# 67 fused pairs in place of 55, and four low parts a group made by an accumulating transfer, in a hybrid encoder layer

## The chip, the cores and the metric

One Trainium2 chip, one core of it. The time of a run is the device time of one execution in microseconds (us). The kernel before takes 1573.97 us, the median of 3 runs (1572.58 to 1574.53). One further execution was taken with the profiler on. Its span, from the first to the last profiled instruction, and its whole time are in the table below.

## The reference

One layer of an encoder: x is 256 rows (tokens) of 4096 numbers, all in float32.

```python
xn = rms_norm(x, norm_g[l])
h = jnp.einsum('bsd,de->bse', xn, w_in[l])              # 4096 -> 7 x 2048
c_val, c_glu, c_gate, q, k, v, a_gate = jnp.split(h, split_pts, axis=-1)
conv_out = conformer_conv(c_val, c_glu, ...) * jax.nn.silu(c_gate)   # 31 taps, LayerNorm, swish
q = rms_norm(q.reshape(B, S, 16, 128), q_norm_g[l])
k = rms_norm(k.reshape(B, S, 16, 128), k_norm_g[l])
attn = longnet_mixture(q, k, v, rel_bias)               # three dilated window patterns
attn_out = attn * jax.nn.silu(a_gate)
mixed = jnp.concatenate([conv_out, attn_out], axis=-1)
x = x + jnp.einsum('bse,ed->bsd', mixed, w_out[l])      # 4096 -> 4096
```

Nearly all of the work is in the two einsums: 256 rows times 4096 x 14336 and times 4096 x 4096 weights, 288 MB of weights that are each used once.

## The kernel before

**Groups and pairs.** The weights are cut into 18 column groups of 1024 columns: 14 "input groups" (numbers 0 to 13) and 4 "out groups" (14 to 17). A group is 16 **pairs**. A pair is two blocks of 128 weight rows by the group's 1024 columns, in SBUF one `raw` tile of 128 x 2048 numbers, 1 MB, loaded by one transfer (`load_pair`, L240) that SyncE (SP) issues. There are `RAW` = 3 raw tiles. The load of the pair three places on is issued when all the steps that read a pair's raw tile have been issued, and it waits for them on the chip. `ORDERS[g]` lists the pairs of group g in the order in which they are done; a place in this list is a "slot", and the number 16 g + slot is the pair's unit u.

**Products.** TensorE multiplies in a reduced-precision format (fp32r here). To keep float32 accuracy each weight is split in a high part (a cast on ScalarE, called ACT in the profile) and a low part (raw minus high, a subtraction on VectorE, DVE), and each activation likewise. A product is three matmuls: high·high, low·high and high·low, 128 x 128 by 128 x 512 each. The sums stay in PSUM over the group's 16 pairs.

**Plain pairs** (`split_plain`, `plain`) need 2 row blocks x 2 halves of the tokens x 2 halves of the columns x 3 = 24 matmuls. ACT casts the high part `wh` in two halves (L1022), and DVE subtracts to get `wl` in one operation (L1028). On TensorE (PE) the 16 matmuls with the high part come first (L1195, L1197), then the 8 with the low part (L1195).

**Fused pairs** (`split_fused`, `fused`) use a Strassen scheme (Winograd's form) on the 2 x 2 blocks: seven products in place of eight, so 7 x 3 = 21 matmuls. It needs sums of weight blocks, made by DVE in the raw tile (L1054, L1063, L1064), and their high and low parts: `b` (L1045, L1046), `b22` (L1061, L1062), and two tiles of sums `t1,t3` and `t2,t4` (L1045, L1046). The block sums of the activations are made once (`block_sums`) and kept in tiles of the tag `c4`, of which there are `C4` = 16. The products of all fused pairs of a group also go to four more accumulators m1, m5, m6, m7, and after the group's last fused pair `add_more` (L1232 to L1240) adds these into the group's output tile: one copy on ACT and eight sums on DVE in an out group. Fused pairs are five in each of the input groups 2 to 7, four in group 14, and seven in each of the groups 15 to 17: 30 + 4 + 21 = 55.

**Parts in store.** The parts wait for PE in `W_SLOTS` = 4 tiles of the tag "ws" (128 x 2048), and near fused pairs in up to `W_MORE` = 4 tiles of tag c4 as well. The class `Stream` holds a list `todo` of splitting steps in the order of the units; `before()`, called ahead of each block of matmuls, issues as many of these steps as there is room for in the tiles. So on ACT and DVE the splitting runs ahead of PE by as much as the store holds.

**Fillers.** The rest (the convolution's taps on DVE, its products on ACT through `cp_lane`, block sums, softmax, gates) is cut into steps, and a planner puts them between the splitting steps. For each matmul `credit()` adds 227 ns times a share `FILL` to what DVE and ACT may spend: (0.95, 0.72) in groups with fused pairs, (0.96, 0.93) while taps are being done elsewhere. Each step says what it costs, and `pump()` starts fillers while something is left.

**Attention.** Softmax tiles are turned by a way through DRAM: GpSimd (POOL) issues the write (L391) and the reads that fetch the turned tiles (L398). The products of the last heads (`po`, L740) stand in the first out group, 14. The weights of the out groups begin with the rows that the attention makes last, by an offset of eight pairs in the row number (in `load_pair`).

**End of a group.** The last pair's matmuls are ordered by accumulator (L1210, L1212), so that the four accumulators are done one after the other. In an out group DVE adds each to the output tile `xr` (L826), which a transfer then writes out.

## Time and profile before

| | us |
|---|---|
| median of 3 runs | 1573.97 |
| the profiled execution, whole | 1575.05 |
| its span | 1573.3 |
| TensorE busy (6901 matmul records) | 1565.2 |
| VectorE busy | 1298.7 |
| ScalarE busy | 928.4 |
| GpSimd busy | 99.2 |
| one raw load of 1 MB, issue to landing (median of 286) | 4.9 |

The profiled execution lies 1.08 us over the median, and 1.75 us of it are outside the span. PE is TensorE's matmul, PEld its weight load, SP is SyncE. A row of the timeline gives the start in us, the duration, the engine, the line of the program, the operation, output<-inputs, the shape and how many alike are in the row; in brackets how long the engine stood idle ahead of it and for what. In a list of waits the three numbers are the sum of the waits in us, their count and the longest. Matmuls are pipelined: one issues every 0.23 us, though each is shown with 0.39. The raw loads are all that SP moves besides x and the output; POOL issues transfers only.

### The profile page before, as it was taken

How to read it: one execution, taken by the hardware profiler on the slowest of the kernel's cores; microseconds unless marked ns; L12 is line 12 of the kernel's file. 1: busy time of each engine (PE TensorE's matmuls, PEld its weight loads, DVE VectorE, ACT ScalarE, POOL GpSimd, SP SyncE). 2: the span in 40 equal slices, each digit the busy share in tenths (PEclk: the TensorE clock that was granted, in tenths of full speed). 3: DMA queues.
4: the chain of work that ended last, by engine and by line, in shares of the span. 5: the costliest groups of instructions: out<-in, count | busy, mean ns of one | idle time of the engine just before them, and what ended most of it. 6: DMA issues, size and time to landing. Idle time of an engine off the chain costs nothing.

```text
span 1573.3 us, 18570 instructions
## 1 busy us (share of the span) xinstructions
PE 1565.2 (99%) x6901; PEld 1294.9 (82%) x6901; DVE 1298.7 (83%) x1473; ACT 928.4 (59%) x1421; POOL 99.2 (6%) x184
## 2 busy tenths in 40 slices
PE   9999999999999999999999999999999999999999
PEld 7888888888888888888888888888888788788887
DVE  6667899998989898898878788767566778989897
ACT  6755655566556555667665776665736644555553
POOL 0000000000000000001203023001130300000000
PEclk9999999999999999999999999999999999999999
DMA  9866556555657565656868469556785865666653
GB/s 373 294 226 259 205 211 223 206 209 196 233 184 249 183 248 203 207 210 236 282 207 257 171 247 280 194 194 212 236 272 200 256 222 205 223 241 228 244 221 136
DMA packets 64523, 357.22 MB, mean 227 GB/s; under 512 B 9104, under 2 KB 11920, under 8 KB 27824
## 3 DMA queue, kind: packets, MB, share of 16 engines
q1 hardware_dynamic: 54096, 326.38, 58.6%
q0 software_dynamic: 10048, 29.37, 6.1%
q8 instruction: 54, 0.88, 0.2%
q10 hardware_dynamic: 288, 0.28, 0.1%
q14 instruction: 37, 0.30, 0.1%
HBM read 337.09 MB, written 18.91 MB: 226 GB/s over the span
## 4 chain that ended last, share of the span: by engine, by line
PE 87%; issue 6%; DMA 4%; DVE 1%; ACT 1%; POOL 0%; SPq 0%; DVEq 0%; POOLq 0%; ACTq 0%
PE c L1195 40%; PE c L1197 20%; PE c L1210 3%; PE m L1082 3%; PE m L1080 3%; PE m L1081 3%; PE c L1080 2%; PE c L1081 2%; PE c L1082 2%; PE acc L927 2%; PE acc L924 2%; PE acc L925 2%; PE c L1212 2%; DMA raw<-in_w_dram 1%; PE psc L696 1%
## 5 line engine op out<-in xcount | busy, mean ns | idle before, releaser
L1028 DVE TENSOR_TENSOR wl<-raw,wh 128x2048 fp32r<-128x2048 f32 x217 | 496.4, 2289 | 174.3 <-ACT wh L1022 165.6
L1022 ACT CAST wh<-raw 128x1024 fp32r<-128x1024 f32 x434 | 433.6, 1048 | 255.4 <-PE c L1197 185.1
L1195 PE MATMUL c<-wh,nh 128*128 128x512 f32 x1200 | 467.4, 390 | 0.0
L1197 PE MATMUL c<-wh,nl 128*128 128x512 f32 x1200 | 466.9, 389 | 0.0
L1195 PE MATMUL c<-wl,nh 128*128 128x512 f32 x1200 | 298.2, 391 | 0.0
L1195 PEld LDWEIGHTS c<-wh,nh 128*128 128x128 f32 x1200 | 225.2, 188 | 46.9
L1195 PEld LDWEIGHTS c<-wl,nh 128*128 128x128 f32 x1200 | 225.3, 188 | 46.7
L1197 PEld LDWEIGHTS c<-wh,nl 128*128 128x128 f32 x1200 | 225.2, 188 | 46.7
L1045 ACT CAST t<-raw 128x1024 fp32r<-128x1024 f32 x110 | 115.9, 1054 | 237.2 <-DVE raw L1054 182.7
L1046 DVE TENSOR_TENSOR t<-raw,t 128x1024 fp32r<-128x1024 f32 x110 | 134.2, 1221 | 2.8
L533 DVE SCALAR_TENSOR_TENSOR cT<-a,wT,cT 128x252 f32<-128x252 f32 (+10 forms) x284 | 117.7, 472 | 0.5
L1195 PE MATMUL c<-wh,mh 128*128 128x512 f32 x280 | 109.1, 390 | 0.0
L1197 PE MATMUL c<-wh,ml 128*128 128x512 f32 x280 | 108.9, 389 | 0.0
L495 ACT ACTIVATE cp<-a,wT 128x241 f32<-128x241 f32 (+7 forms) x196 | 84.5, 488 | 9.9 <-DVE cT L524 9.8
L1195 PE MATMUL c<-wl,mh 128*128 128x512 f32 x280 | 69.1, 389 | 0.0
L1054 DVE TENSOR_TENSOR raw<-raw 128x1024 f32<-128x1024 f32 x55 | 67.4, 1225 | 1.9
L1046 DVE TENSOR_TENSOR b<-raw,b 128x1024 fp32r<-128x1024 f32 x55 | 67.0, 1218 | 0.2
L1195 PEld LDWEIGHTS c<-wh,mh 128*128 128x128 f32 x280 | 52.6, 188 | 10.9
L1197 PEld LDWEIGHTS c<-wh,ml 128*128 128x128 f32 x280 | 52.6, 188 | 10.9
L1195 PEld LDWEIGHTS c<-wl,mh 128*128 128x128 f32 x280 | 52.6, 188 | 10.9
L998 DVE TENSOR_TENSOR wh<-raw,wh 128x1024 fp32r<-128x1024 f32 x31 | 37.9, 1224 | 24.8 <-ACT wh L997 24.8
L524 DVE TENSOR_TENSOR cT<-cT,cp 128x964 f32<-128x964 f32 (+7 forms) x49 | 57.1, 1166 | 1.1
(327 smaller groups left out, 2170.6 us busy)
## 6 DMA issues: line engine op xcount, KB each, us to landing
raw<-in_w_dram SPq DMA_DIRECT2D x286, 1024.0 KB, 4.9
xT<-in_x_cols_dram SPq DMA_DIRECT2D x15, 512.0 KB, 8.0
x<-in_x_dram SPq DMA_DIRECT2D x8, 512.0 KB, 8.8
xr<-in_x_dram SPq DMA_DIRECT2D x8, 512.0 KB, 6.5
out_dram<-xr SPq DMA_DIRECT2D x15, 256.0 KB, 6.8
T<-bias_dram SPq DMA_DIRECT2D x16, 192.0 KB, 6.1
raw<-in_w_dram SPq DMA_DIRECT2D x3, 512.0 KB, 6.7
turn_qk0d<-turn_qk POOLq DMA_DIRECT2D x2, 512.0 KB, 5.5
```

The lines of the kernel that those rows point to most:

```text
L495: nc.scalar.activation(cp[:, t, lo:hi], a[:, t, lo + sh : hi + sh], AF.Copy, scale=wT[:, 4 * cb + t, k : k + 1],)
L533: nc.vector.scalar_tensor_tensor(c[:, t, lo:hi], a[:, t, lo + sh : hi + sh], wT[:, 4 * cb + t, k : k + 1], c[:, t, lo:hi], op0=ALU.mult, o ...
L1022: nc.scalar.copy(h, raw_tiles[u][:, k])
L1028: nc.vector.tensor_sub(l, src, h.bitcast(F32))
L1045: nc.scalar.copy(h, src)
L1046: nc.vector.tensor_sub(l, src, h.bitcast(F32))
L1054: nc.vector.tensor_add(r[:, 0:4:3, :], r[:, 0:3:2, :], twice(r[:, 3, :]))
L1080: nc.tensor.matmul(acc, a[0], b[0], start=start, stop=False)
L1081: nc.tensor.matmul(acc, a[1], b[0], start=False, stop=False)
L1082: nc.tensor.matmul(acc, a[0], b[1], start=False, stop=stop)
L1195: nc.tensor.matmul(acc, a[s][0], b[e], start=begin, stop=False)
L1197: nc.tensor.matmul(acc, a[s][1], b[e], start=False, stop=False)
```

## The change

Three things change, and several smaller ones follow from them.

1. **More fused pairs.** In the input groups 2 to 7 pair 12 becomes fused as well (six a group), and in the out groups 15 to 17 pairs 0 to 7 and 9 (nine a group in place of seven): 36 + 4 + 27 = 67. The new pair's block sums use two tiles of a smaller tag (`small`), and `C4` rises to 18, which also holds the two tiles that the convolution's products had for themselves.
2. **Low parts by a transfer.** In the last three groups pairs 10, 11, 12 and 13 are split by `split_by_dma`. The high part is cast as before. The low part is not subtracted on DVE: ACT writes the negated value of raw, rounded to fp32r, into `wl` (L1046 of the new program), and GpSimd issues a transfer that reads the same weights from DRAM again and adds them to it (L1048), in two halves of 512 KB. That is 12 pairs, 24 negations and 24 transfers. PE multiplies the high part after the next fused pair and the low part after the one behind that (`late`). The splitting steps are taken into those of the neighbouring fused pairs (`guest`, `held`).
3. **Order in a fused pair.** The four products of t1 to t4 are done with all high parts first, then with the low parts.

Besides: `add_more` is a row of steps, one taken behind each half of a plain part, where it was done at once; `FILL` rises; the store may hold 7 more tiles in the out groups 15 to 17 (`W_LAST`); the ACT products of the convolution are started behind the `b22` cast where ACT has credit.

```diff
-FILL, SAVED = ((0.95, 0.72), (0.96, 0.93)), (700, 700)
+FILL, SAVED = ((0.97, 0.76), (1.0, 0.93)), (700, 700)
-C4 = 16
+C4 = 18
-FUSED = [(2, 4, 6, 8, 10) if g in FUSED_IN else () for g in range(N_IN)]
-FUSED += [range(4)] + 3 * [range(7)]
+FUSED = [(2, 4, 6, 8, 10, 12) if g in FUSED_IN else () for g in range(N_IN)]
+FUSED += [range(4)] + 3 * [(*range(8), 9)]
-ORDERS += 3 * [(8, 9, 0, 10, 1, 11, 2, 3, 12, 4, 5, 13, 6, 14, 15, 7)]
-W_SLOTS, W_MORE = 4, 4
+ORDERS += 3 * [(8, 10, 0, 1, 11, 2, 3, 12, 4, 5, 13, 6, 7, 9, 14, 15)]
+BY_DMA = (N_IN + 1) * [()] + 3 * [(10, 11, 12, 13)]
+W_SLOTS, W_MORE, W_LAST = 4, 4, 7
...
-    cps = deque((const.tile([P, 4, S], F32, name=f"cp{i}"), 0) for i in range(2))
+    cps = deque((t4(f"cp{i}"), 0) for i in range(2))
...
-        if left[1] > 1500 and not split_gens:
+        if left[1] > 1500 and state["taps"] and not split_gens:
             cp_lane.step(left, spend)
...
+                elif ORDERS[g][slot] in BY_DMA[g]:
+                    make = self.split_by_dma
                 new = [(n, f, u) for n, f in make(u)]
                 self.parts_left[u] = len(new)
+                if make == self.split_by_dma:
+                    guest = new
+                    continue
+                if guest:
+                    new[2:] = [*guest[:2], new[2], guest[2], new[3]]
+                new[1:1], held, guest = held, guest[3:], []
                 self.todo.extend(new)
...
+        def split_by_dma(self, u):
+            g, slot = divmod(u, n_pairs)
+            def low(k):
+                if k == 0:
+                    self.parts[(u, "l")] = self.two(f"wl{u}", (u, "l"))
+                l = self.parts[(u, "l")][k]
+                nc.scalar.activation(l, raw_tiles[u][:, k], AF.Copy, scale=-1.0)
+                src = w[g, row_of(u), :, 1024 * k : 1024 * k + 1024]
+                nc.gpsimd.dma_start(l, src.bitcast(F32R), accum_op=ALU.add)
+                spend(0, 1055)
+            halves = (TWO, lambda: low(0)), (NONE, lambda: low(1))
+            return [*self.split_plain(u)[:2], *halves]
...
                 nc.scalar.copy(h, r[:, 2, :])
+                for _ in range(2):
+                    if left[1] > 800:
+                        cp_lane.step(left, spend)
                 nc.vector.tensor_sub(l, r[:, 2, :], h.bitcast(F32))
...
+                more_now = W_LAST if g > n_in else W_MORE
+                self.more = more_now if firsts and slot + 2 >= firsts[0] else 0
...
                     if last:
-                        self.add_more(g, more)
+                        self.adding = self.add_more(g, more)
+                    if late and late[0] >= u - 2:
+                        self.plain(*late, rows, one, False, "hl"[u - late[0] - 1])
                     continue
...
+                if j in BY_DMA[g]:
+                    late = u, j
+                    continue
...
-                (more["m5"], "s1", "t1", ""), (more["m7"], "s3", "t3", "t13"),
-                (more["m6"], "s2", "t2", ""), (one["c21"], "a22", "t4", "t42"),
...
+            for part in range(2):
+                for acc, an, bn in sums:
+                    self.before()
+                    own = acc is not one["c21"]
+                    (ah, al), b = a[an], self.parts[(u, bn)][part]
+                    begin, end = own and first and part == 0, own and last and part == 1
+                    nc.tensor.matmul(acc, ah, b, start=begin, stop=end)
+                    if part == 0:
+                        nc.tensor.matmul(acc, al, b, start=False, stop=False)
+                    credit((2 - part) * PRODUCT)
```

How this moves the instructions is seen at three places. The first is ACT in the last three groups. Before, in group 17, two fused pairs (units 278 and 279) are followed by a plain one, whose two `wh` casts stand behind all of the fused pairs' casts:

```order
L1045 CAST b_11541<-raw_11463 128x1024
L1061 CAST b_278_11546<-raw_11463 128x512
L1045 CAST t_278_11560<-raw_11463 128x1024
L1045 CAST t_278_11569<-raw_11463 128x1024
L1045 CAST b_11590<-raw_11502 128x1024
L1061 CAST b_279_11594<-raw_11502 128x512
L1045 CAST t_279_11607<-raw_11502 128x1024
L1045 CAST t_2790_11616<-raw_11502 128x1024
L1022 CAST wh_11631<-raw_11533 128x1024 x2
L1045 CAST b_11654<-raw_11572 128x1024
```

After, in group 15, with the by-DMA pair in raw_10434 (unit 247) and the fused pairs 248, 249 and 251 in raw_10423, raw_10465 and raw_10537:

```order
L1084 CAST b_10477<-raw_10423 128x1024
L1100 CAST b_248_10483<-raw_10423 128x512
L1061 CAST wh_10504<-raw_10434 128x1024 x2
L1084 CAST t_2480_10513<-raw_10423 128x1024
L1046 ACTIVATE wl_10520<-raw_10434 128x1024
L1084 CAST t_248_10534<-raw_10423 128x1024
L1084 CAST b_10541<-raw_10465 128x1024
L1046 ACTIVATE wl_10521<-raw_10434 128x1024
L1100 CAST b_249_10562<-raw_10465 128x512
L1084 CAST t_249_10573<-raw_10465 128x1024
L1084 CAST t_2490_10589<-raw_10465 128x1024
L1084 CAST b_10597<-raw_10537 128x1024
```

The by-DMA pair's casts and its two negations now stand inside the splitting of the two fused pairs, and POOL issues the transfer of a half as soon as its negation is done.

The second place is PE inside a fused pair, in the sums t (before, unit 278 of group 17; m are the four more accumulators, msp and mh/ml the parts of the activations):

```order
L1080 MATMUL m_17_11458<-t_278_11560,msp_9626 128x512
L1081 MATMUL m_17_11458<-t_278_11560,msp_9626 128x512
L1082 MATMUL m_17_11458<-t_278_11560,msp_9626 128x512
L1080 MATMUL m_17_11460<-t_278_11560,msp_9626 128x512
L1081 MATMUL m_17_11460<-t_278_11560,msp_9626 128x512
L1082 MATMUL m_17_11460<-t_278_11560,msp_9626 128x512
L1080 MATMUL m_17_11459<-t_278_11569,msp_9626 128x512
L1081 MATMUL m_17_11459<-t_278_11569,msp_9626 128x512
L1082 MATMUL m_17_11459<-t_278_11569,msp_9626 128x512
L1080 MATMUL c_17_11378<-t_278_11569,mh_9592 128x512
L1081 MATMUL c_17_11378<-t_278_11569,ml_9593 128x512
L1082 MATMUL c_17_11378<-t_278_11569,mh_9592 128x512
```

After (unit 251 of group 15; t_2510 holds the high parts of t1 and t3, t_2511 their low parts, t_251 both parts of t2 and t4):

```order
L1237 MATMUL m_15_10327<-t_2510_10631,msp_9855 128x512
L1239 MATMUL m_15_10327<-t_2510_10631,msp_9855 128x512
L1237 MATMUL m_15_10329<-t_2510_10631,msp_9855 128x512
L1239 MATMUL m_15_10329<-t_2510_10631,msp_9855 128x512
L1237 MATMUL m_15_10328<-t_251_10651,msp_9855 128x512
L1239 MATMUL m_15_10328<-t_251_10651,msp_9855 128x512
L1237 MATMUL c_15_10275<-t_251_10651,mh_9821 128x512
L1239 MATMUL c_15_10275<-t_251_10651,ml_9822 128x512
L1237 MATMUL m_15_10327<-t_2511_10632,msp_9855 128x512
L1237 MATMUL m_15_10329<-t_2511_10632,msp_9855 128x512
L1237 MATMUL m_15_10328<-t_251_10651,msp_9855 128x512
L1237 MATMUL c_15_10275<-t_251_10651,mh_9821 128x512
```

The first matmul that needs a low part was the third of these twelve (L1082) and is now the ninth; the first that needs the t2,t4 tile was the seventh and is now the fifth.

The third place is PE at the last heads of the attention, in group 14. Before, the products of the heads' four tiles `pr` stand in one row:

```order
L1195 MATMUL c_14_9542<-wh_9695,mh_9117 128x512
L1197 MATMUL c_14_9542<-wh_9695,ml_9118 128x512
L740 MATMUL po_9754<-pr_9174,agv_1_9524 128x256 x2
L740 MATMUL po_9757<-pr_9179,agv_1_9524 128x256 x2
L740 MATMUL po_9760<-pr_9204,agv_1_9524 128x256 x2
L740 MATMUL po_9763<-pr_9220,agv_1_9524 128x256 x2
L1195 MATMUL c_14_9543<-wh_9695,mh_9115 128x512
```

After, the first three stand at the same place in the group, and the last one (pr_9286) here:

```order
L1267 MATMUL c_14_9608<-wh_9776,mh_9257 128x512
L1269 MATMUL c_14_9608<-wh_9776,ml_9258 128x512
L754 MATMUL po_9866<-pr_9286,agv_1_9584 128x256 x2
L1267 MATMUL c_14_9605<-wl_9787,mh_9255 128x512
L1267 MATMUL c_14_9606<-wl_9787,mh_9255 128x512
```

Between them are 32 matmuls of plain pairs that were behind all four before.

More of the change, by code (lines that the diff above doesn't have):

```diff
@@ L544, in conv_gen @@
         conv_done[cb] = True
+        if cb == 3:
+            cps.clear()
     fetched = set()
@@ L1174, in fused @@
                     self.free((u, freed))
+            sums = (
+                (more["m5"], "s1", "t1"), (more["m7"], "s3", "t3"),
+                (more["m6"], "s2", "t2"), (one["c21"], "a22", "t4"),
+            )
+            for part in range(2):
[8 more added lines that the diff above has]
+                    credit((2 - part) * PRODUCT)
+                    if part == 1 and bn == "t3":
+                        self.free((u, "t13"))
+            self.free((u, "t42"))
+            for _, _, bn in sums:
+                del self.parts[(u, bn)]
         def blocks_of(self, u, j, rows, part):
@@ L1183, in blocks_of, with plain @@
                     [[t[:, P * s : P * s + P] for t in a] for s in range(2)],
-                    [w[:, 1024 * k + 512 * e : 1024 * k + 512 * e + 512] for e in range(2)],
+                    [wk[:, 512 * e : 512 * e + 512] for e in range(2)],
                 )
-        def plain(self, u, j, rows, one, first):
-            for part in "hl":
+        def plain(self, u, j, rows, one, first, parts="hl"):
+            for part in parts:
                 for e in range(2):
@@ L1218, in add_more @@
             u = t2(f"us{g}")
-            if groups[g][0] != "out":
+            into = groups[g][0] == "out"
+            if into:
+                r = [[xr_tiles[(g, e)][:, s, :] for e in range(2)] for s in range(2)]
+                m1, v = t2(f"m1s{g}"), t2(f"vs{g}")
+            else:
                 for e in range(2):
```

83 lines of the change are left out of this document (51 added, 32 removed).

## The prediction

> **What bounds the kernel now.** I read the page's head first, then PE's waits, then the windows by stage, then the timelines of the engines that feed PE.
>
> ```profile
> span 1573.3 us, 18570 instructions
> PE 1565.2 (99%) x6901; PEld 1294.9 (82%) x6901; DVE 1298.7 (83%) x1473; ACT 928.4 (59%) x1421; POOL 99.2 (6%) x184
> ```
>
> TensorE is busy for all but 8.1 us of the span. PE's list of waits has four entries:
>
> ```profile
> PE po L740 <- DMA pr<-turn_p15d: 1.7, 1, 1.7
> PE m L1082 <- DVE t L1046: 1.3, 1, 1.3
> PE spin L1256 <- DVE ones L163: 1.1, 1, 1.1
> PE acc L924 <- ACT wh L997: 0.2, 1, 0.2
> ```
>
> The last two stand in the program's first group, which the change leaves alone; the first two, 3.0 us together, stand where it acts. So PE sets the time, and fewer matmuls is time, as long as nothing begins to keep PE waiting. How near are the others? These windows are six input groups with fused pairs (the first row) and the last three out groups (one row each); the columns are window, length, busy time of PE, PEld, DVE, ACT and POOL with their instruction counts, PE's granted clock, the DMA engines' share and GB/s:
>
> ```profile
> 181.00:441.00 260.00, 260.00 (x1149) 215.29 (x1148) 236.49 (x243) 149.24 (x196) 1.65 (x3) 1.00 0.58 206
> 1322.00:1405.00 83.00, 81.70 (x360) 66.96 (x359) 77.01 (x75) 41.74 (x47) 0.00 (x0) 1.00 0.64 231
> 1405.00:1487.00 82.00, 82.00 (x363) 67.92 (x362) 74.85 (x70) 42.95 (x48) 0.00 (x0) 1.00 0.64 231
> 1487.00:1573.30 86.30, 82.47 (x364) 67.94 (x362) 73.56 (x71) 40.99 (x45) 0.00 (x0) 0.99 0.52 192
> ```
>
> (The first window is about three of the six input groups.) VectorE is the second bound, at 0.91 of PE in both stages; ScalarE is half idle; the clock is full, so a matmul saved is saved at full speed.
>
> **The change, part by part.**
>
> *Matmuls removed.* A plain pair has 24, a fused one 21; 12 more pairs are fused, so 36 go. In the chain of waits one plain pair of 24 lies between these two rows:
>
> ```profile
> 97.81 2.04 PE c L1195 x9
> ...
> 103.25 2.04 PE c L1195 x9
> ```
>
> That is 5.44 / 24 = 0.2267 us each (the window 1405:1487 says the same: 82.00 / 363 = 0.226). **36 × 0.2267 = 8.16 us less.** The other parts decide how much of it arrives.
>
> *VectorE in the last three groups.* Its timeline there, first a run of eight small sums into the output tiles and two subtractions of plain pairs, then one fused pair up to the start of the next:
>
> ```profile
> 1389.77 0.68 DVE L1233 TENSOR_TENSOR xr<-xr,m 128x512 f32<-128x512 f32 x1
> ...
> 1394.69 4.49 DVE L1028 TENSOR_TENSOR wl<-raw,wh 128x2048 fp32r<-128x2048 f32 x2
> ...
> 1445.31 1.22 DVE L1046 TENSOR_TENSOR b<-raw,b 128x1024 fp32r<-128x1024 f32 x1
> 1446.56 1.23 DVE L1054 TENSOR_TENSOR raw<-raw 128x1024 f32<-128x1024 f32 x1
> 1447.70 0.69 DVE L1062 TENSOR_TENSOR b<-raw,b 128x512 fp32r<-128x512 f32 x1
> 1448.42 0.69 DVE L1063 TENSOR_TENSOR raw<-raw 128x512 f32<-128x512 f32 x1
> 1449.14 0.69 DVE L1064 TENSOR_TENSOR raw<-raw 128x512 f32<-128x512 f32 x1
> 1449.75 2.43 DVE L1046 TENSOR_TENSOR t<-raw,t 128x1024 fp32r<-128x1024 f32 x2
> 1452.10 1.22 DVE L1046 TENSOR_TENSOR b<-raw,b 128x1024 fp32r<-128x1024 f32 x1
> ```
>
> A fused pair takes VectorE 1452.10 − 1445.31 = 6.79 us, a plain one 4.49 / 2 = 2.25, the sums 1394.69 − 1389.77 = 4.92, and the four of the group's end 4 × 0.68 = 2.7. Before: 7 × 6.79 + 9 × 2.25 + 4.92 + 2.7 = 75.4 us a group. After: nine fused, and only three plain pairs subtract on VectorE: 9 × 6.79 + 3 × 2.25 + 4.92 + 2.7 = 75.5. PE has 357 × 0.2267 = 80.9 in place of 82.3. So the four by-DMA pairs pay for the two new fused ones, and 5.4 us of slack a group stay. In the steady pattern (two fused, one by-DMA) PE takes 66 × 0.2267 = 14.96 and VectorE 13.58.
>
> *ScalarE there.* Each by-DMA pair adds two negations (a copy of a 128x1024 half, taken as the cast of that shape, about 1.05 us as in the rows below): 8.4 us a group on an engine busy 43 of 82. They go into gaps:
>
> ```profile
> 1447.89 1.05 ACT L1045 CAST t<-raw 128x1024 fp32r<-128x1024 f32 x1 [3.36 <-DVE raw L1054]
> 1449.87 1.05 ACT L1045 CAST t<-raw 128x1024 fp32r<-128x1024 f32 x1 [0.92 <-DVE raw L1064]
> 1450.83 1.05 ACT L1045 CAST b<-raw 128x1024 fp32r<-128x1024 f32 x1
> 1450.98 0.39 PE L1080 MATMUL m<-b,mh 128*128 128x512 f32 x1
> ```
>
> The first negation stands between the two casts of t (an idle 0.92 for 1.05, so t comes 0.13 late), the second behind the next b cast, ahead of the b22 cast. That cast's result is wanted by VectorE only 2.39 us after the b cast's (1447.70 − 1445.31), and it takes 0.6 itself: 1.05 more fits. Cost taken: nothing.
>
> *The transfers.* The low half is issued when its negation ends. VectorE's block that starts at 1445.31 is multiplied from 1450.98 (the PE row above). On that scale the first negation ends about 1450 (cast at 1447.89, then two of 1.05), 1 us before PE starts the pair, the second about 1453, 2 us behind. PE then runs a fused pair, the by-DMA pair's high part (16 matmuls) and a second fused pair, 58 × 0.2267 = 13.15 us, before it wants the low part. So a half may take about **11 us** to land, the first one 14. What it does take no row shows: there is no accumulating transfer before. The nearest rows are GpSimd's 0.5 MB writes, and the weight loads alone and beside such traffic (last column: median us to landing):
>
> ```profile
> raw<-in_w_dram SPq DMA_DIRECT2D x16, 1024.0 KB, 4.8
> raw<-in_w_dram SPq DMA_DIRECT2D x3, 1024.0 KB, 8.2
> turn_qk1d<-turn_qk POOLq DMA_DIRECT2D x2, 512.0 KB, 8.4
> turn_qk0d<-turn_qk POOLq DMA_DIRECT2D x1, 512.0 KB, 5.9
> raw<-in_w_dram SPq DMA_DIRECT2D x6, 1024.0 KB, 9.6
> ```
>
> The first row is from 1320:1400 with no GpSimd traffic, the next three from 733:750, the last from 920:960. I take 6 to 9 us for an accumulating half: below 11, no cost. Bounds: below, 5 us, nothing to gain; above, see the rival.
>
> *What the transfers do to the loads.* In the pattern fused, fused, by-DMA, the raw buffer that the next first fused pair needs comes free when VectorE ends the pattern's first fused pair; VectorE then has 6.79 us of the second one, and a b cast of 1.05 must precede its next work. So a load may land in 6.79 − 1.05 = 5.74 us for nothing; now it lands in 4.8, and after the change both accumulating halves are in flight beside it. Above 5.74 VectorE idles, three times a group; its slack is 5.4 us a group, so a group loses 3 × (L − 5.74) − 5.4 us: nothing at 7.5, 2.0 at 8.2, 6.2 at 9.6. I take 7 to 8, and **2 us in all** for it and the start of each group, where VectorE has no lead yet; ends 0 and 18.6 (3 × 6.2).
>
> *The order inside a fused pair.* The four t products now do their eight high matmuls first, then the four low ones. The stall of 1.3 us is here, in the first of the three last out groups:
>
> ```profile
> 1359.26 0.50 PE L1082 MATMUL m<-t,msp 128*128 128x512 f32 x1
> ```
>
> It is the third matmul of the t's; the first low part is now wanted at the ninth, 6 × 0.2267 = 1.36 us later. But the last low part (t2, t4), one 1.22 later on VectorE, is wanted two matmuls after that, 0.45, so with the same lateness about 0.7 is left. **0.6 less**; bounds 0 and 1.3.
>
> *The attention's last head.* The wait of 1.7:
>
> ```profile
> 1252.06 2.17 POOL L398 DMA_DIRECT2D pr<-turn_p15d  x4 [3.88 <-DMA turn_p15d<-turn_p]
> 1254.47 2.75 PE L740 MATMUL po<-pr,agv 128*128 128x256 f32 x12
> 1258.87 1.10 PE L740 MATMUL po<-pr,agv 128*128 128x256 f32 x4 [1.65 <-DMA pr<-turn_p15d]
> ```
>
> All four last products stood together, some 110 matmuls into the first out group. By the order of the program the last one now stands 32 matmuls further back, 7.3 us of PE, apart from the other three. **1.7 less**; bounds 0 and 1.7.
>
> *The input groups.* Six groups get a sixth fused pair and a more daring planner. One fused pair for a plain one gives VectorE 6.79 − 2.25 = 4.54 us more; the first window is 236.49 / 260 us over 260 / (369 × 0.2267) = 3.1 groups, 76.1 a group, so 80.6 of PE's 366 × 0.2267 = 83.0: 0.97, with 2.4 us of slack a group. The plain subtractions wait for their cast, which is to say VectorE is ahead:
>
> ```profile
> 456.27 2.29 DVE L1028 TENSOR_TENSOR wl<-raw,wh 128x2048 fp32r<-128x2048 f32 x1 [0.68 <-ACT wh L1022]
> 466.90 2.29 DVE L1028 TENSOR_TENSOR wl<-raw,wh 128x2048 fp32r<-128x2048 f32 x1 [1.07 <-ACT wh L1022]
> ```
>
> A plain and a fused pair come every 10.63 us, with 1.07 idle, and PE takes 45 × 0.2267 = 10.20. Idle here can shrink, so I take nothing. The convolution's taps and block sums are put between these pairs:
>
> ```profile
> L533 DVE SCALAR_TENSOR_TENSOR cT<-a,wT,cT 128x252 f32<-128x252 f32 (+10 forms) x284 | 117.7, 472 | 0.5
> L524 DVE TENSOR_TENSOR cT<-cT,cp 128x964 f32<-128x964 f32 (+7 forms) x49 | 57.1, 1166 | 1.1
> ```
>
> Where they crowd, a group can be late by two or three of them: bounds 0 and 12 (2 us in each of six groups).
>
> *Sum.* 1575.05 (the profiled execution, 1573.3 of it span) − 8.16 − 0.6 − 1.7 + 2.0 = 1566.6. The median of the runs is 1573.97, 1.08 below the profiled one: **1565.5 us**, 8.5 below before.
>
> **The rivals.**
>
> *Raw loads land late (B).* As worked out above. For it: 8.2 and 9.6 beside GpSimd's traffic. Against: those rows hold much smaller pieces beside the 0.5 MB writes. At L of 8.2 it costs 5.9, in place of my 2: 1569.4; at 9.6, 18.6, and 1582.
>
> [...]
>
> *The transfers are slow (C, the other side).* The DMA engines are busy 0.64 of 82 us, 52.5, for about 18 MB: 2.9 us a MB. Four MB more a group at the price of a copy are 11.7 us, and the share is (52.5 + 11.7) / 80.9 = 0.79. At twice the price 0.94, and from 2.4 times the engines are full: at three times a group takes 52.5 + 35 = 87.5, 6.6 over PE's 80.9, 20 us in three groups, 1583. The same happens by latency: beyond 11 us each of the 12 pairs makes PE wait for its low part, 12 × (landing − 11); 12 us landing eats the gain (12 × 1 = 12), 13 gives 1587. It decides where a half lands: below 11 nothing, above 11.8 the kernel is slower than before.
>
> [...]
>
> *VectorE fills up in the input groups (D).* 0.97 on average, with fillers put in by credit, not evenly; 1 to 2 us in each of six groups: 1571 to 1577. For: 2.4 us of slack a group against pieces of 0.47 and 1.17 us. Against: the idle 0.68 and 1.07.
>
> *It does not do what it says (E).* The last head's wait moves or grows with the later convolution, and stalls come in at the out groups' starts: 4 to 7 of the 8 us given back, 1570 to 1574.
>
> **How the numbers follow.** Forecast 0.58 (1562 to 1569), B 0.14 (1568 to 1582), C 0.12 (1575 to 1590 and more), D 0.11 (1569 to 1577), E 0.05. The least is the whole gain with no new wait, 1575.05 − 8.16 − 3.0 − 1.08 = 1562.8, and the runs of before spread to 1.4 below their median: low end 1561.5. The top, 1577, takes in D and most of B and leaves out C; what is left out is about 0.15. A measurement tells about 0.2% (3.1 us) from no change, so faster is below 1570.8: the forecast, half of B, over half of D, a little of E: 0.71. Same (to 1577.1): 0.13. Slower: C and the worst of B, 0.16.
>
> **What the next profile would show.** Right: 36 matmuls fewer, PE's waits a few us in all, the accumulating halves landing below 11 us, no wait of a plain low part's matmuls for a DMA, VectorE 0.97 in the input groups, the last head without a wait. Raw loads of the last three groups at 7 to 8 us, and VectorE's b subtractions waiting for them. Wrong: matmuls of the low parts released by a DMA (C), VectorE idle for raw and PE idle for VectorE's t or b in the last three groups (B), PE waiting for VectorE between 100 and 600 us (D).

## The result and the profile after

| | before | after |
|---|---|---|
| median, us | 1574.49 (5 runs, 1572.58 to 1575.19) | 1624.75 (5 runs, 1622.05 to 1626.0) |
| span of the profiled execution, us | 1573.3 | 1622.2 |
| raw load of 1 MB in the last three groups, median us to landing | 4.9 | 8.3 |

Two further runs of the kernel before are in its median here.

The ratio is 1.0318, with a 95% interval of 1.0307 to 1.033: the changed kernel is 50 us slower, where 8.5 us faster was forecast, and 48 us above the top of the range. Its page begins:

```profile
span 1622.2 us, 18704 instructions
PE 1578.1 (97%) x6865; PEld 1293.5 (80%) x6865; DVE 1335.3 (82%) x1608; ACT 939.3 (58%) x1392; POOL 120.0 (7%) x208
```

The 36 matmuls are gone (6901 records before, 6865 after), and still PE is busy 13 us longer. Where the time lies is read from the last pair of each group, whose matmuls with the low part have a line of their own. The rows give count, shortest, median and longest duration, and the start of the first and of the last. Before (the first row for the groups 2 to 13, the second for 14 to 17):

```profile
L1210 PE MATMUL c<-wl,nh x96: 389/389/390, 260.5 to 1230.7; 128*128 128x512 f32 x96
L1210 PE MATMUL c<-wl,mh x32: 388/389/389, 1316.1 to 1569.1; 128*128 128x512 f32 x32
```

After:

```profile
L1283 PE MATMUL c<-wl,nh x96: 389/389/499, 261.5 to 1232.4; 128*128 128x512 f32 x96
L1283 PE MATMUL c<-wl,mh x32: 388/389/389, 1316.0 to 1617.0; 128*128 128x512 f32 x32
```

The input groups end 1.7 us later than before, although they have 18 matmuls fewer. Group 14 takes 1.8 less, so the last three groups start level. From there to the end it takes 301 us in place of 253: **the loss is made in the last three groups, some 48 us of it**, and the input groups gain nothing.

PE's waits after:

```profile
PE c L1267 <- DMA wl<-in_w_dram: 20.2, 9, 3.4
PE m L1237 <- ACT t L1084: 8.0, 13, 1.2
PE c L1283 <- DVE wl L1067: 3.7, 2, 2.1
PE m L1122 <- DVE xr L840: 3.4, 3, 2.4
PE c L1267 <- DVE wl L1067: 1.4, 1, 1.4
```

The first two and the fourth are in the last three groups; the first is the wait for the new transfers. The third and the fifth, 5.1 us together, are in the input groups. The windows of the last three groups show what the waits do not:

```profile
1312.00:1410.00 98.00, 86.67 (x352) 68.32 (x351) 73.12 (x78) 52.86 (x58) 6.98 (x8) 0.95 0.72 225
1410.00:1510.00 100.00, 88.93 (x364) 69.42 (x363) 76.04 (x79) 55.12 (x62) 6.92 (x8) 0.97 0.74 235
1510.00:1610.00 100.00, 89.27 (x366) 69.87 (x365) 76.69 (x80) 54.26 (x60) 6.93 (x8) 0.97 0.72 227
```

A group takes about 99 us. VectorE's work in it is 76, as worked out; the DMA engines are busy 0.73 of it, in all 72 us; the granted clock is no longer full (0.95 to 0.97). So neither VectorE nor the DMA engines are full over a group, and PE stands idle for 33 us of the three windows. Who waits for the loads is told by the waits of ScalarE and VectorE in the whole run:

```profile
ACT b L1084 <- DMA raw<-in_w_dram: 55.4, 16, 7.2
DVE b L1085 <- ACT b L1084: 48.5, 13, 7.1
ACT wh L1061 <- DMA raw<-in_w_dram: 27.6, 16, 4.0
```

Before, no b cast waited for a load, and the `wh` casts waited 4.9 us. The chain of waits in two patterns of the second of these groups (a pattern is one by-DMA pair and two fused ones) shows the loads:

```profile
1430.45 12.26 DMA raw<-in_w_dram
...
1449.89 11.37 DMA wl<-in_w_dram
...
1474.38 10.92 DMA raw<-in_w_dram
...
1487.42 11.82 DMA raw<-in_w_dram
```

These are three raw loads that take 11 to 12 us, and a transfer that takes as long. Queues and issues in the same group, 1410 to 1510 (queue: packets, MB, share of the 16 engines; issue: count, KB, median us to landing; the queues' MB are 10^6 bytes, so a raw load is 1.05 of them):

```profile
q1 hardware_dynamic: 3472, 19.27, 50.6%
q0 software_dynamic: 1152, 4.19, 23.5%
...
raw<-in_w_dram SPq DMA_DIRECT2D x16, 1024.0 KB, 8.3
wl<-in_w_dram POOLq DMA_DIRECT2D x8, 512.0 KB, 8.8
```

A MB of raw loads and outputs holds the engines 50.6 / 19.27 = 2.63 us, a MB of the accumulating transfers 23.5 / 4.19 = 5.6 us, 2.1 times as long. Now rows of one pattern, of VectorE, ScalarE and GpSimd:

```profile
1447.66 1.23 DVE L1085 TENSOR_TENSOR t<-raw,t 128x1024 fp32r<-128x1024 f32 x1 [0.55 <-ACT t L1084]
...
1458.42 1.23 DVE L1085 TENSOR_TENSOR b<-raw,b 128x1024 fp32r<-128x1024 f32 x1 [2.74 <-ACT b L1084]
...
1464.36 1.22 DVE L1085 TENSOR_TENSOR t<-raw,t 128x1024 fp32r<-128x1024 f32 x1 [1.41 <-ACT t L1084]
```

```profile
1448.48 1.05 ACT L1046 ACTIVATE wl<-raw 128x1024 fp32r<-128x1024 f32 x1
...
1457.34 1.05 ACT L1084 CAST b<-raw 128x1024 fp32r<-128x1024 f32 x1 [2.92 <-PE c L1239]
...
1461.39 2.00 ACT L1061 CAST wh<-raw 128x1024 fp32r<-128x1024 f32 x2 [2.48 <-DMA raw<-in_w_dram]
1463.29 1.04 ACT L1084 CAST t<-raw 128x1024 fp32r<-128x1024 f32 x1
...
1467.08 1.06 ACT L1046 ACTIVATE wl<-raw 128x1024 fp32r<-128x1024 f32 x1
```

```profile
1447.05 0.89 POOL L1048 DMA_DIRECT2D wl<-in_w_dram  x1 [17.33 <-ACT wl L1046]
1449.89 0.87 POOL L1048 DMA_DIRECT2D wl<-in_w_dram  x1 [1.95 <-ACT wl L1046]
```

The raw tile of the by-DMA pair is free when its second negation ends, at 1449.5. Its next load, issued then, takes 11.8 us and lands at 1461.3. ACT stands still for it, and the t cast of the fused pair is behind the two `wh` casts in its row; so VectorE stands too, 1.41 us. From the landing to the end of the next second negation, which frees the tile again, ACT needs 6.8 us (1461.3 to 1468.1). Landing and work, 11.8 + 6.8 = 18.6 us, are the length of this pattern, where PE's work is 14.96.

The tile of the pattern's first fused pair comes free at nearly the same time, 1448.9 (VectorE's end of it). Its load takes 8.3 us and lands at 1457.2, the b cast follows at 1457.34, and VectorE has stood 2.74 us for that. (The row names a PE matmul as the last that this cast waited for; that matmul ended 0.1 us behind the landing.) The transfers are issued at 1447.1 and 1449.9. So within 3 us the engines get two loads of 1 MB and two halves of 512 KB that count double, as much as four loads: 4 × 1.05 × 2.63 = 11.0 us of all sixteen, an estimate from the prices above, and near the 11.8 us of the load. From 1462.5 to 1465.9 the DMA engines are nearly empty (a share of 0.02), until the next tiles come free.

PE, when the low part lands late, and the granted clock (the last but two of the numbers) in two windows of 5 us there:

```profile
1461.30 1.95 PE L1267 MATMUL c<-wl,mh 128*128 128x512 f32 x6 [2.63 <-DMA wl<-in_w_dram]
1463.05 0.63 PE L1122 MATMUL m<-b,mh 128*128 128x512 f32 x1
1463.47 0.63 PE L1123 MATMUL m<-b,ml 128*128 128x512 f32 x1
...
1465.98 0.39 PE L1123 MATMUL c<-b,msp 128*128 128x512 f32 x1
1466.21 0.39 PE L1124 MATMUL c<-b,msp 128*128 128x512 f32 x1
```

```profile
1455.00:1460.00 5.00, 3.67 (x17) 2.70 (x15) 2.22 (x3) 1.57 (x2) 0.00 (x0) 1.00 1.04 323
1460.00:1465.00 5.00, 3.70 (x11) 2.94 (x12) 3.52 (x5) 3.61 (x4) 0.00 (x0) 0.75 0.47 196
```

After the wait of 2.63 us the matmuls come every 0.42 us (1463.47 − 1463.05) in place of 0.23, until 1466, and the granted clock of that window is 0.75: in the trace it is 0.5 for 3.41 us, from 1462.5 on. By that the half clock costs 3.41 / 2 = 1.7 us more than the wait itself. The same 3.41 us stand seven times in the last three groups, which makes 12 us lost, each behind a wait of PE of 2.17 us or more; behind two other waits of the run, of 2.07 and 2.21 us, they are missing. What decides between the two was not shown. PE's 33 us of idle time and these 12 are most of what the last three groups lost: 48 us, and 4 more that 18 matmuls fewer should have brought.

### The profile page after: what moved, and what is told of

It is laid out like the page before. It is cut to its first block, busy times and chain, and to the rows that moved or that the text cites. A ratio compares the mean times of both kernels' runs of the same rounds, so it can differ in the third digit from the quotient of the medians.

```text
span 1622.2 us, 18704 instructions
## 1 busy us (share of the span) xinstructions
PE 1578.1 (97%) x6865; PEld 1293.5 (80%) x6865; DVE 1335.3 (82%) x1608; ACT 939.3 (58%) x1392; POOL 120.0 (7%) x208
## 4 chain that ended last, share of the span: by engine, by line
PE 79%; DMA 9%; issue 4%; DVE 4%; ACT 2%; POOL 0%; SPq 0%; DVEq 0%; ACTq 0%; POOLq 0%
PE c L1267 37%; PE c L1269 18%; DMA raw<-in_w_dram 7%; PE m L1237 3%; PE c L1283 3%; PE acc L941 2%; PE acc L938 2%; PE acc L939 2%; PE m L1239 2%; PE c L1285 1%; DMA wl<-in_w_dram 1%; PE c L1237 1%; PE c L1124 1%; PE c L1123 1%; PE c L1122 1%
## 5 line engine op out<-in xcount | busy, mean ns | idle before, releaser
L1067 DVE TENSOR_TENSOR wl<-raw,wh 128x2048 fp32r<-128x2048 f32 x193 | 441.4, 2289 | 139.7 <-ACT wh L1061 135.6
L1061 ACT CAST wh<-raw 128x1024 fp32r<-128x1024 f32 x410 | 409.3, 1048 | 243.9 <-PE c L1269 144.1
L1269 PE MATMUL c<-wh,nl 128*128 128x512 f32 x1152 | 448.2, 389 | 0.0
L1084 ACT CAST t<-raw 128x1024 fp32r<-128x1024 f32 x134 | 140.8, 1050 | 225.4 <-DVE raw L1093 164.4
L1085 DVE TENSOR_TENSOR t<-raw,t 128x1024 fp32r<-128x1024 f32 x134 | 163.3, 1221 | 18.6 <-ACT t L1084 15.9
L545 DVE SCALAR_TENSOR_TENSOR cT<-a,wT,cT 128x255 f32<-128x255 f32 (+14 forms) x364 | 150.1, 471 | 0.3
L1084 ACT CAST b<-raw 128x1024 fp32r<-128x1024 f32 x67 | 70.2, 1048 | 60.5 <-DMA raw<-in_w_dram 55.4
L1267 PE MATMUL c<-wl,mh 128*128 128x512 f32 x232 | 63.8, 413 | 20.2 <-DMA wl<-in_w_dram 20.2
L1237 PE MATMUL m<-t,msp 128*128 128x512 f32 x186 | 64.4, 400 | 8.0 <-ACT t L1084 8.0
L1237 PE MATMUL m<-t,xsp 128*128 128x512 f32 x180 | 60.3, 389 | 0.0
L507 ACT ACTIVATE cp<-a,wT 128x241 f32<-128x241 f32 (+4 forms) x116 | 49.2, 488 | 10.5 <-DVE cT L536 10.5
```

Source lines behind the costliest of these rows:

```text
L507: nc.scalar.activation(cp[:, t, lo:hi], a[:, t, lo + sh : hi + sh], AF.Copy, scale=wT[:, 4 * cb + t, k : k + 1],)
L545: nc.vector.scalar_tensor_tensor(c[:, t, lo:hi], a[:, t, lo + sh : hi + sh], wT[:, 4 * cb + t, k : k + 1], c[:, t, lo:hi], op0=ALU.mult, o ...
L1061: nc.scalar.copy(h, raw_tiles[u][:, k])
L1067: nc.vector.tensor_sub(l, src, h.bitcast(F32))
L1084: nc.scalar.copy(h, src)
L1085: nc.vector.tensor_sub(l, src, h.bitcast(F32))
```

## The experiments

Two theories stood at the start. **Loads theory:** the transfers lie beside the raw loads, which come late, and with three raw tiles that makes each pattern about 18.7 us long in place of 15.0. **Order theory:** the by-DMA pair's casts and negations in ACT's row hold up the t casts, whatever the transfers do. The first four runs change the transfers.

**1. All low parts on VectorE.**

```diff
-BY_DMA = (N_IN + 1) * [()] + 3 * [(10, 11, 12, 13)]
+BY_DMA = (N_IN + 4) * [()]
```

> Loads theory (the 24 accumulating transfers lie beside the raw loads, so that each pattern of two fused and one by-DMA pair takes 18.7 us in place of 15.0): without the transfers the patterns run at the pace of DVE, which then has 9 x 6.79 + 7 x 2.25 + 7.6 = 84.5 us a group against 80.9 of PE; the last three groups take about 254 us in place of 301, so 1578 (1574 to 1583). Order theory (the casts and negations of the by-DMA pair stand in ACT's row ahead of the t casts and hold them up, whatever the transfers do): the casts still stand near the fused pair, so part of the loss stays, 1590 or more.

Measured: 1590.6 us (ratio 1.0103, 1.0088 to 1.0118). 34 us of the loss are gone. That is above the range of the loads theory and at the low end of the order theory's, so it does not decide. All low parts on VectorE cost more than its busy time: with 84.5 us a group that would be 254, and the stretch of the last three groups (as in the rows above) takes 268 us, 15 more than before.

**2. The last three groups as before.**

```diff
-FUSED += [range(4)] + 3 * [(*range(8), 9)]
-ORDERS += 3 * [(8, 10, 0, 1, 11, 2, 3, 12, 4, 5, 13, 6, 7, 9, 14, 15)]
-BY_DMA = (N_IN + 1) * [()] + 3 * [(10, 11, 12, 13)]
-W_SLOTS, W_MORE, W_LAST = 4, 4, 7
+FUSED += [range(4)] + 3 * [range(7)]
+ORDERS += 3 * [(8, 9, 0, 10, 1, 11, 2, 3, 12, 4, 5, 13, 6, 14, 15, 7)]
+BY_DMA = (N_IN + 4) * [()]
+W_SLOTS, W_MORE, W_LAST = 4, 4, 4
```

> The last three groups as before (seven fused pairs, no by-DMA pair), the input groups and the order of high and low parts as changed. Both theories: the loss was made in the last three groups alone, so 1573 (1570 to 1576): the input groups with six fused pairs ended 1.7 us later than before in the profile, the attention's last head no longer waits (1.7 less). If the new order inside the fused pairs or the input groups cost something that the profile hides: above 1577.

Measured: 1575.94 (ratio 1.0009, 0.9999 to 1.0018). So the loss is in the last three groups, and 18 matmuls fewer in the input groups bring nothing. This is the base of the runs 5 and 11 to 16.

**3. The transfers copy, and do not add.**

```diff
-                nc.gpsimd.dma_start(l, src.bitcast(F32R), accum_op=ALU.add)
+                nc.gpsimd.dma_start(l, src.bitcast(F32R))
```

> The transfers are there, from the same place with the same bytes, but copy in place of adding (the low parts are then the raw weights). In the profile an accumulated MB held the DMA engines 5.7 us against 2.6 for a MB of raw loads. Loads theory: the bunch of two loads and two transfers shrinks from 4 to 3 MB's worth, landings from about 11.5 to 8.5 us, the pattern from 18.7 to 15 to 16 us: 1575 to 1590. Order theory: no change, 1620 or more.

Measured: 1601.99 (1.0172, 1.0155 to 1.0189), above the range. The queues between 1330 and 1430 us, and one issue:

```profile
q1 hardware_dynamic: 4055, 20.38, 55.1%
q0 software_dynamic: 1376, 5.05, 17.8%
```

```profile
1368.02 0.54 POOL L1048 DMA_DIRECT2D wl<-in_w_dram  x1 [2.29 <-ACT wl L1046]
```

A copied MB holds the engines 17.8 / 5.05 = 3.5 us, not 2.6, and the raw loads land in 7.2 (median). Of the loss, 23 us hang on the addition; the other 27 come with a mere copy of the same bytes. Why a copied MB is dearer than a loaded one was not tested: the queue and the length of a row (4 KB against 8 KB) differ at once.

**4. No transfers.**

```diff
-                src = w[g, row_of(u), :, 1024 * k : 1024 * k + 1024]
-                nc.gpsimd.dma_start(l, src.bitcast(F32R), accum_op=ALU.add)
```

> The negations stay and the 24 transfers are left out (the low parts are then the negated raw weights). Loads theory: raw loads land in 5 us again, the last three groups take PE's 3 x 80.9 + the stretches at the starts, some 249 us in place of 301: 1573 (1570 to 1577). Order theory: the rows of ACT and DVE are the same, so 1610 or more.

Measured: 1574.44 (0.9997, 0.9988 to 1.0006): all 50 us are gone, with every cast and negation in its place, and the raw loads land in 4.8 us again (median). This settles between the two theories: the transfers make the loss; ACT's row alone does not. (PE's wait for the transfers' landing goes with them; the runs 6 and 7 are about that.) Two windows of this run, and PE's wait in the first:

```profile
1316.00:1399.00 83.00, 80.57 (x349) 66.26 (x348) 75.35 (x80) 54.72 (x60) 0.00 (x0) 0.98 0.60 229
1399.00:1482.00 83.00, 83.00 (x367) 68.72 (x367) 76.02 (x81) 54.72 (x61) 0.00 (x0) 1.00 0.61 231
```

```profile
PE m L1120 <- DVE xr L840: 2.4, 1, 2.4
```

In the second window PE is never idle, at full clock, with VectorE at 76.0, as the prediction had it. And yet the kernel is no faster than before, and the 8.2 us of the 36 matmuls are gone in two places. The last three groups take 251.3 us, 1.7 less than before and not 4.1: at the start of group 15 PE waits 2.4 us for VectorE's four sums of group 14's end, which now stand behind a fused pair's first five operations on VectorE and stood ahead of a plain pair's subtraction before. The first window's granted clock is 0.98 of 83 us, as much as 3.41 us at half clock make, an estimate: 1.7 us. The changed kernel has the same wait (the fourth in its list). The input groups are the second question.

The next three runs ask how the transfers act.

**6. Both negations directly behind the casts.**

```diff
-                    new[2:] = [*guest[:2], new[2], guest[2], new[3]]
-                new[1:1], held, guest = held, guest[3:], []
+                    new[2:] = [*guest, new[2], new[3]]
+                new[1:1], held, guest = held, [], []
```

> The changed kernel with both negations of a by-DMA pair directly behind its two casts. The raw tile of that pair is free after 2.0 + 2.1 us of ACT's work in place of about 7.2 (three other casts no longer lie between). If the by-DMA pair's own loop (landing 11.5 + 7.2 = 18.7 us) sets the pattern: 12 patterns, each up to 3 us shorter, 1590 to 1605. If the loads of the fused pairs, which land as late, set it as well (their loop: landing 11 + a cast of 1.05 + 6.8 of DVE = 18.9): 1615 to 1626.

Measured: 1613.23 (1.0245, 1.0227 to 1.0262), 11.5 us better and outside what either case had. The loop of the by-DMA pair's tile is part of it, not all: between 1330 and 1560 us ScalarE's `wh` casts, which waited 19.3 us for raw tiles in the changed kernel, are gone from the list of those that wait for them, but its b casts still wait there, 42.1 us in place of 47.4. Two of PE's waits:

```profile
PE m L1237 <- ACT t L1084: 14.4, 9, 1.6
...
PE c L1267 <- DMA wl<-in_w_dram: 1.9, 3, 1.2
```

The wait for the transfers falls from 20.2 to 1.9 us, since they are issued earlier, and the time falls by 11.5 only: the wait goes over to the fused pair's parts, which hang on the loads.

**7. The low part multiplied one fused pair later.**

```diff
-            more = late = None
+            more, late = None, []
...
-                    if late and late[0] >= u - 2:
-                        self.plain(*late, rows, one, False, "hl"[u - late[0] - 1])
+                    for n, (lu, lj) in enumerate(late):
+                        seen = sum(ORDERS[g][k - g * n_pairs] in FUSED[g] for k in range(lu, u + 1))
+                        if seen in (1, 3):
+                            self.plain(lu, lj, rows, one, False, "h" if seen == 1 else "l")
...
-                    late = u, j
+                    late.append((u, j))
```

(and `W_LAST` = 9.)

> The changed kernel with the low part of a by-DMA pair multiplied one fused pair later, behind the third in place of the second (7 to 9 us more room for a transfer, and two more tiles for it in store). If PE's waits for the transfers themselves (20.2 us in the profile, the rival C of the prediction) make the time: 1600 to 1608. Loads theory: the transfers' lateness is only where PE happens to stand while the raw loads are late; the waits move to the fused pairs' parts, 1616 to 1626.

Measured: 1635.28 (1.0387, 1.0372 to 1.0403), 10.5 us worse. The wait for the transfers is gone from the list; in its place stands, with 30.7 us,

```profile
PE m L1239 <- ACT t L1084: 30.7, 17, 6.5
```

So more room for a transfer brings nothing. The loads theory had foreseen the place of the waits, not that they would grow: the low parts hold their store longer, and what that displaces was not looked into.

**9. Two by-DMA pairs a group.** `BY_DMA` has pairs 11 and 13 only.

> The changed kernel with two by-DMA pairs a group (11 and 13) in place of four; the lows of 10 and 12 are DVE's. Loads theory, each pattern by itself: none of them gives 1590.6, four 1624.75, so two 1607 (1602 to 1612). If a pattern without transfers lets the loads recover and the next one starts with a lead: 1590 to 1600. DVE has 80.0 us a group against PE's 80.9, so without any effect of the transfers it would be about 1577.

Measured: 1614.61 (1.0255, 1.0239 to 1.027): above the middle between none (1590.6) and four (1624.75). The first two pairs cost 24 us, the next two 10, though each also takes 2.25 us from VectorE. The raw loads land in 6.2 us (median) and PE waits 15.0 us for the transfers.

The other runs ask why the smaller gains did not come.

**10. The order in a fused pair alone**, put into the kernel before.

> The kernel before, with nothing changed but the order inside a fused pair: the high matmuls of the four sums first, then the low ones. The prediction took 0.6 us for it; in the changed kernel PE waits for the high cast of t2 and t4 (8.0 us), which is now wanted as the fifth in place of the seventh of the twelve. 1573.4 (1572.5 to 1574.5) by the prediction; above 1575 if the earlier need of that cast costs more than the later need of the low parts saves.

Measured: 1575.18 (1.0001, 0.9993 to 1.001): nothing. PE's wait of 1.3 us for a low part has become one of 1.2 for the high cast:

```profile
PE m L1183 <- ACT t L1045: 1.2, 2, 0.9
```

**5 and 8. The old FILL.** Run 5 is run 2 with `FILL` = ((0.95, 0.72), (0.96, 0.93)); run 8 has this too, eight fused pairs (0 to 7) in each of the last three groups, and no transfers.

> As the run with the last three groups as before (1575.9), and the planner's shares FILL at their old values too. Filler theory (the three waits of PE for plain low parts, 5.1 us in the input groups, are there because DVE is given up to 1.00 of PE's time for fillers where it was 0.96): those waits go, 1571 (1569 to 1573). If the sixth fused pair itself fills DVE: the waits stay, 1575 to 1577, or new ones come where the convolution ends later.

> No transfers: eight fused pairs in each of the last three groups, all low parts on DVE, six fused pairs in the input groups, FILL at its old values. 27 matmuls fewer than before, 6.1 us. DVE has 8 x 6.79 + 8 x 2.25 + 7.6 = 79.9 us a group and PE 360 x 0.2267 = 81.6, so PE still sets the pace: 1567 (1565 to 1571). If DVE in the steady stretches is already too late (each fused pair in a row of two gives back its lead): 1572 to 1578.

Measured: 1600.08 (1.0164, 1.0149 to 1.018) and 1603.66 (1.0187, 1.0171 to 1.0202). Both times lie far above what was expected, though the first expectation had named new waits of a late convolution. The waits for plain low parts did go, and the input groups ended at 1225.7 us in run 5, 5.0 earlier than before. But work of the convolution and the attention was put off, and group 14 had to wait for it:

```profile
PE po L754 <- DMA pr<-turn_p12d: 15.3, 1, 15.3
PE c L1267 <- ACT mh L786: 4.4, 1, 4.4
```

So at lower shares VectorE's fillers are late at the end, and at higher ones (run 2) they hold up plain pairs. In run 8 the stretch of the last three groups takes 256.6 us, 3.6 more than with seven fused pairs before, although it has 9 matmuls fewer and VectorE's sum, 79.9 a group, is below PE's 81.6. Why it falls short with those 1.7 us of slack was not tested.

**11, 12, 15, 16. Other shares** on run 2: `FILL` for VectorE in groups with fused pairs and in the others 0.97 and 0.96 (run 11), 0.97 and 0.98 (12), 1.00 and 1.00 (15), 1.00 and 0.98 (16).

> As the run with the last three groups as before, with the new FILL (0.97, 0.76) in the groups with fused pairs and the old one (0.96, 0.93) in the others. PE's three waits (5.1 us) stand in groups without fused pairs, where FILL went from 0.96 to 1.00. If these waits come from that share and the rest of the work is early enough: 1571 (1569 to 1573). If the work that is not done there is late for the attention, as with the old shares: 1580 to 1600.

> The same with (0.98, 0.93) in the groups without fused pairs: half of the way. Waits in the input groups between 0 and 5 us, and the attention's tail late by less than half of what the run before this one shows: 1572 to 1585. Below 1572.5 it would beat the kernel before.

> As the run with the last three groups as before, with FILL (1.00, 0.80) in the groups with fused pairs, where PE never waited, and (1.00, 0.93) in the others. If work moves into the fused groups: fewer waits later, 1572 to 1575. If DVE is full there: PE waits between 185 and 700 us, 1576 to 1580.

> The same with (0.98, 0.93) in the others. The run with 0.97 and 0.98 gave 1580.4, 5.9 of it waits for the attention's tiles. If the fused groups take up more: 1571 to 1576; if not: 1580.

Measured: 1590.72 (1.0098, 1.0081 to 1.0116), 1580.38 (1.0035, 1.0021 to 1.0048), 1575.37 (1.0009, 0.9999 to 1.0018) and 1575.80 (1.0008, 0.9998 to 1.0017). With the one for the others at 0.98, a higher share in the fused groups brings 4.6 us (run 16 against 12); none is below the kernel before.

**13 and 14. The old rule for the convolution's products.** Run 2 with

```diff
-        if left[1] > 1500 and state["taps"] and not split_gens:
+        if left[1] > 1500 and not split_gens:
```

and in run 14 `FILL` as in run 11. The rule of the change leaves fewer products on ACT. The first row is before, the other three are after:

```profile
L495 ACT ACTIVATE cp<-a,wT 128x241 f32<-128x241 f32 (+7 forms) x196 | 84.5, 488 | 9.9 <-DVE cT L524 9.8
```

```profile
L545 DVE SCALAR_TENSOR_TENSOR cT<-a,wT,cT 128x255 f32<-128x255 f32 (+14 forms) x364 | 150.1, 471 | 0.3
L507 ACT ACTIVATE cp<-a,wT 128x241 f32<-128x241 f32 (+4 forms) x116 | 49.2, 488 | 10.5 <-DVE cT L536 10.5
L536 DVE TENSOR_TENSOR cT<-cT,cp 128x964 f32<-128x964 f32 (+4 forms) x29 | 33.8, 1166 | 1.2
```

80 products went from ACT to VectorE as taps: 150.1 − 117.7 = 32.4 us more there, less the sums of products that fall away (57.1 − 33.8 = 23.3), 9 us net.

> As the run with the last three groups as before (1575.9), with the old rule for the convolution's products on ACT (also in groups with fused pairs wherever ACT has credit). If DVE's 80 additional taps make the waits: DVE is 9 us freer, the three waits of 5.1 us shrink below 2, 1572 (1570 to 1574). If the waits come from the share that the planner may give: still about 1576.

> The same, with 0.96 for the groups without fused pairs (with the new rule for the products: 1590.7, the attention came late). If the 9 us of DVE were what made it late: 1571 to 1574. If the share decides: 1585 or more.

Measured: 1582.79 (1.0052, 1.0035 to 1.0069) and 1577.89 (1.0025, 1.0015 to 1.0035). In run 14 the old rule is worth 13 us against run 11: the 9 us of VectorE are much of what made the attention late at that share. In run 13, at the high share, it loses 7 us against run 2. Where it loses them is seen in the fused groups, in the first row for run 2, in the second for run 13:

```profile
185.00:700.00 515.00, 515.00 (x2274) 426.44 (x2273) 477.42 (x517) 280.24 (x366) 6.02 (x11) 1.00 0.58 212
185.00:700.00 515.00, 512.56 (x2235) 417.21 (x2234) 472.20 (x467) 308.16 (x439) 6.04 (x11) 1.00 0.58 208
```

PE does 39 matmuls fewer in the same time, 8.8 us' worth, in short delays, most of them at the sums t; run 14 has 36 fewer there too, and run 2 has no such delay. ScalarE has 28 us more work in that window, so its products probably hold up the t casts; that is not shown. Rule and shares belong together, and no pair of them that was tried brings the 4.1 us.

## Why the prediction was wrong, by its own steps

- **What the transfers do to the loads: this step failed.** The prediction followed one tile, that of the pattern's first fused pair, whose load may take 5.74 us for nothing; it took 7 to 8 us and put in 2 us for all three groups. In the pattern above this load took 8.3 us, and by the prediction's formula that is 3 × (8.3 − 5.74) − 5.4 = 2.3 us a group; a group became 18 us longer. What it left out is the by-DMA pair's own tile: its load is issued together with the other one and with the transfers, took 11.8 us, and with 6.8 us of ACT's work made the pattern 18.6 us long, where the sum has 14.96. Three such patterns are 11 us a group. About 4 more are the clock, which the sum took as full. The range took 9.6 us, a median of another place in the program, as its worst. It should have added up what is issued in one bunch: 2 MB of loads at 2.63 us a MB and 1 MB of transfers at 5.6.
- **The transfers' price.** Rival C gave "at twice the price 0.94", and twice it was (5.6 us a MB against 2.63). A half was taken to land in 6 to 9 us: median 8.8, with those that PE waited for around 11. But a share of the engines is a mean, and a mean below one was taken as room (0.73 in the windows above). With three raw tiles the loads did not use the time between the bunches: run 4 against the changed kernel shows 50 us for the transfers. A fourth raw tile was not tried.
- **PE's wait for the low parts** (rival C) is there, 20.2 us, on transfers of 11 us. In the runs 6 and 7 it is nearly or wholly gone, and the time moved by −11.5 and +10.5; both change something else as well, but it can't be more than a part of the 50 us.
- **ScalarE in gaps, no cost.** Right without the transfers (run 4). With them the `wh` casts wait for the late load in ACT's row, ahead of the fused pair's t cast, which the prediction did not see.
- **VectorE's 75.5 us a group:** 76.0. **Matmuls:** right, 36 fewer.
- **The start of each group** was in the 2 us with the loads, and rival E named stalls there: the wait of 2.4 us and the half clock behind it, by the estimate above 4.1 us in run 4, as much as the 18 matmuls of the last three groups.
- **The attention's last head:** 1.7 expected, 1.8 measured in group 14 (in run 2 it is back with 1.5, so it hangs on the finer timing).
- **The order in a fused pair:** 0.6 expected, nothing measured (run 10). The high cast of t2 and t4 is wanted earlier by as much.
- **The input groups:** the 4.1 us of 18 matmuls were counted as gained with no cost; PE waits 5.1 us there for plain low parts, 1.6 of them in group 1 and 3.5 behind the fused groups. The prediction had looked for VectorE's limit in the fused groups, where PE never waits. The fillers that the sixth fused pair displaces, and the products that moved from ACT to VectorE, which it left out, come up in the groups around them. The runs 5, 11, 12 and 14 change VectorE's share or its work and move the loss between the input groups and the attention, so it hangs on VectorE; the new shares with five fused pairs were not run, so the sixth pair and the shares are not told apart.

## What to carry to other kernels

A transfer that replaces work of an engine is not priced by its landing alone, nor by a mean share of the DMA engines: add up what is issued at the same moment, with each kind of transfer at its measured price (here 5.6 us a MB for an adding one, 2.63 for a raw load), and follow each buffer's loop, landing plus the work that frees it, against the length of the pattern. Work that is taken from an engine's slack in one stage comes back where its fillers are due; look for that stage, and count what a change of a rule moves between engines. A wait of PE can cost more than itself: seven of the nine waits over 2 us in the changed kernel were followed by 3.4 us at half clock.

## What was not expected of the hardware

- A MB that a transfer adds to SBUF held the DMA engines 5.6 us, a MB copied by the same queue 3.5 (run 3), a MB of raw loads 2.6. GpSimd's issue of an adding transfer took 0.87 us, of a copy 0.54.
- After PE idle of 2.6 us the matmuls came every 0.42 us in place of 0.23, with the granted clock at 0.50 for 3.41 us; after the idle 1.65 us of the kernel before they came every 0.23 from 1260.04 on, at a clock of 1.00.
